# Other tiles for early weights and for the MLP's low halves in an encoder kernel

## The chip, the cores and the metric

The kernel runs on one core of a Trainium2 chip. The metric is the device time of one execution in microseconds. Five engines work side by side, each through its own queue of instructions in a fixed order: TensorE (PE, matmuls; PEld is its weight load), VectorE (DVE), ScalarE (ACT), GpSimd (POOL) and SyncE (SP), which issues most DMAs here. POOL issues some too. An instruction that waits holds up everything behind it on its engine.

## The reference

One encoder layer over two token groups (1024 and 256 tokens, 1280 in all, handled together), width 1024, all in float32:

```python
n = rms_norm(h, g_mix)
z = n @ w_in                      # columns: qa ka va (differential attention), qb kb vb (grouped queries)
oa = diff_attention(qa, ka, va)   # 4 heads, two softmax maps each, distance penalty, sub-norm
ob = gqa_attention(rope(norm(qb)), rope(norm(kb)), vb)   # 8 query heads, 2 kv heads
h = h + concat(oa, ob) @ w_out
a = relu(rms_norm(h, g_mlp) @ w_ff1); h = h + (a * a) @ w_ff2
h = h + sigmoid(rms_norm(h, g_ple) @ w_ple_gate) * (p @ w_ple_proj)
y = rms_norm(h, g_final)
```

## The kernel before, in words

Every float32 operand of a large matmul is split into a high and a low half (`hi` by a rounding copy on ACT, `lo` by a subtraction on DVE or POOL), and a product is three matmuls: high by high, high by low, low by high.

**Start.** `load_w` fetches 256 columns of `w_in` in four chunks of 256 KB (`raw`, shown as rawp in the profile), splits each (L185 on ACT, L186 on DVE), and returns the halves. Two chunks share one tile of SBUF: K0 or K1, taken in turn by the counter `raw_k`. A tile is given to its next user when its last reader is done. The first unit's weights are `w_kv`, the second's `w_va0`; later come `w_b0`, `w_va1` and one more. `load` chains its DMAs on SP: each is issued behind the one before. The chain runs: the four chunks of w_kv with pieces of x for the first 256 tokens between them (xr, and two in the tiles of xt), the four chunks of w_va0, two xt loads for the norm's statistics, two xr loads for tokens 256 to 511 (`load_x`, split at L265 and L266), then small tables. The program interleaves the matmuls of the two units, `b_unit` (psb) and `va_unit` (psv), 256 tokens at a time. Somewhat later `early_w1` uses Q0 and Q1 for the first columns of `w_ff1` (w1e).

**Attention.** Keys lie in K0, K1, Q0 and a tile of the attention pool. Finished outputs pass through the tiles o, or and ml of the pool `late`: `mixed_out` splits the last result into ml (L587 on ACT, L591 on POOL) and stores it to DRAM (md<-ml, L592). The output projection runs beside attention as side work: it loads 128 tokens of the outputs (mt<-md, L892), multiplies (pso), and adds the result to the residual (L940 on DVE). Its second half goes on when attention has ended, over four PSUM banks.

**The MLP's input.** After each norm (`mlp_norm`: L988 store, L998 to L1014) `mlp_transpose` turns 128 tokens (trn, L1103) and copies them to tiles nb (L1111 on ACT). The first matrix product of the MLP uses a scheme of seven products in place of eight, so `mlp_sums` makes seven inputs, in order 1, 6, 7, 4, 5, 2, 3: some are tiles nb as they stand, four are sums (L1135 on DVE). The first sum, t3, goes to tile T2 and the second, t2, to a tile nt; the others go to spare columns of the residual tiles (h_sb). Each input i then reaches its tile Li (`LO[i]`, shown as nlo), in one of two ways: the first groups of 128 tokens by a copy that POOL issues as DMA (L1118), later ones, from `DIRECT` on, by a split straight from the source (`n_split`, L1197 on ACT, L1198 on DVE). What was copied is split in place afterwards, by `first(i)`.

**Where tiles lie.** The pools on the left side are a stack: Q0 and Q1; then K0 and K1 (1280 words a partition each); then, during attention, `late` (o 768, or 256, ml 512 words) and the rest of the attention tiles. When attention ends, K0, K1 and all attention tiles are dropped, and the MLP's pools are stacked on the same ground: W9 (1024 words) and T2 (512), then L1 to L7 (2560 each), then W10, W11 and others. A new tile's first write waits until the tiles beneath it are done with, transfers included.

**Order.** The order of instructions on each queue is fixed when the program is built, by a simulated timeline that takes what is ready, earlier-written work first. The order written in the program is therefore not always the order on the queue, and any change of a wait can alter it elsewhere. `issue_after` holds chosen instructions behind others.

Of the kernel before, what the change touches and what calls it, by code (L numbers as in the profile page):

```python
# [14 lines left out]
F32 = mybir.dt.float32  # L15
# [8 lines left out]
P = 128  # L24
# [16 lines left out]
def f(ap):  # L41
    return ap.bitcast(F32)
# [3 lines left out]
def encoder_kernel(ctx: ExitStack, tc: tile.TileContext, x, xT, pT, w_in, w_out, w_ff1, w_ff2, w_gate, w_proj,  # L46
# [49 lines left out]
    def pool(name, bufs=1, side=None, space=None, stack=None):  # L96
        kw = dict(name=name, bufs=bufs, reuse_waits="tile")
        if side:
            kw["side"] = side
        if space:  # L100
            kw["space"] = space
        return (stack or ctx).enter_context(tc.tile_pool(**kw))
# [54 lines left out]

    w_dma = []
    raw_k = itertools.count()
    WHB = 11  # L160
    EVERY = 3
    FETCH = ((4, 6), (5, 7), (6, 2), (8, 5))
# [3 lines left out]
    def load_w(src, cols, n, rawp, wp, tag, lo_eng, between={}, dma=dma):  # L166

        c0 = cols
        hi, lo = [], []
        kn = 512 // n  # L170
        kw = {"bufs": WHB} if n == 256 else {}
        for kk in range(KD // kn):
            if kk in between:
                between[kk]()
            if n == P:
                raw = rawp.tile([P, kn, n], F32, tag="raw", name=f"raw{tag}", bufs=2)[:]
            else:

                if kk % 2 == 0:
                    raws = slot(f"K{next(raw_k) % 2}", [P, 2, kn, n], F32, f"raw{tag}")  # L180
                raw = raws[:, kk % 2]
            w_dma[:] = [dma(raw, src[kk * kn * P:(kk + 1) * kn * P, c0:c0 + n].rearrange("(k p) c -> p k c", p=P))]
            a = wp.tile([P, kn, n], F32R, tag="wh", name=f"wh{tag}", **kw)
            b = wp.tile([P, kn, n], F32R, tag="wl", name=f"wl{tag}", **kw)
            S.activation(a, raw, AF.Copy)  # L185
            lo_eng.tensor_tensor(b, raw, f(a[:]), op=ALU.subtract)  # L186
            hi += [a[:, i, :] for i in range(kn)]
            lo += [b[:, i, :] for i in range(kn)]
        return hi, lo
# [4 lines left out]
    def slot(tag, shape, dt, name):  # L194
        return slot_pool[tag].tile(shape, dt, tag=tag, name=name, bufs=1)

    def open_slots(pool_, tags):
        for tag in tags:
            slot_pool[tag] = pool_
            size = {"H": 2560, "L": 2560, "W": 1024, "Q": 1280, "K": 1280, "T": 512}[tag[0]]  # L200
            slot(tag, [P, size], F32, tag)
# [22 lines left out]
    def pj(name):  # L224
        return ppj.tile([P, 512], F32, tag="pj", name=name)
# [177 lines left out]
    def qk_a(h):  # L403

        for c, dst, sc in ((512 + P * h, kd[h], 1.0), (P * h, qd[h], -0.125 / SLOPES[h])):
            w = load_w(w_in, c, P, rawp, wp, "a", G, dma=load)
            yield from qk_unit(dst, sc, w)

    def wload(c, between={}, dma=dma):
        return load_w(w_in, c, 256, bp, bp, "p", V, between, dma)  # L410
# [541 lines left out]
    def side_work():  # L952
        yield from qk_rest()
        flush()
        open_out_proj()
        chs2 = (2, 3, 6, 7)
        ahead = []
        for ch in chs2[:2]:
            box = []
            ahead.append(lambda ch=ch: w_next.append(opw_split(opw_dma(ch))))  # L960
        yield from out_proj((0, 1, 4, 5), [], ahead, [pj], True)
        yield from out_proj(chs2, w_next, None, banks2, False)
# [63 lines left out]
    side = side_work()  # L1026
# [42 lines left out]
    pp2.append(pool("pp2", space=PSUM, bufs=1))  # L1069
    bank = lambda tag, name: pj(name) if tag == "pj" else pp2[0].tile([P, 512], F32, tag=tag, name=name, bufs=2)  # L1070
    banks2.append(lambda name: bank("f2", name))
    open_slots(pool("flz", side="left"), ["W9", "T2"])
    open_slots(pool("fl", side="left"), [f"L{i}" for i in range(1, 8)])
    HSLOT = {1: 0, 6: 1, 7: 2, 5: 3, 4: 5, 2: 6, 3: 4}
    open_slots(pool("fw", side="left"), ["W10", "W11"])
    LO = {i: slot(f"L{i}", [P, 4, HT], F32R, f"nlo{i}") for i in range(1, 8)}
# [466 lines left out]
    for ti, t in enumerate(FORD):  # L1543
# [70 lines left out]
        i = 2 if last else 1  # L1614
# [11 lines left out]
        for n0 in range(0, 512 if last else D, 512):  # L1626
            n = slice(n0, n0 + 512)
# [54 lines left out]
```

## Time and profile before

| | |
|---|---|
| median of three runs | 1716.8 us (1715.22 to 1717.41) |
| the profiled execution | 1716.65 us, of which the span is 1714.7 us |
| mean granted TensorE clock | 0.996 |
| busy share of the span | PE 97%, DVE 69%, ACT 51%, POOL 39% |
| bytes moved by DMA | 278 MB, mean 162 GB/s |

A row of the timeline reads: start in us, duration, engine, line of the program, operation, output<-inputs, shapes, count, and in brackets the time the engine stood idle before it and what ended that. A releaser is inferred: where it had long been done, another one, often a DMA, was the last. The windows give, for a stretch, the busy time of each engine, the granted clock of TensorE (1.00 is full), the mean busy share of the 16 DMA engines and the rate. The chain of waits is followed back from the last instruction.

### The profile page before, as it was taken

The numbers are of one execution on the slowest core, as the hardware profiler recorded it, in microseconds if no ns is written. First come the engines' busy times: TensorE is split into PE (matmuls) and PEld (weight loads), VectorE is DVE, ScalarE is ACT, GpSimd is POOL, SyncE is SP. The second block draws the span as 40 slices with busy tenths as digits, with TensorE's granted clock in tenths as the row PEclk, the third lists the DMA queues.
The fourth block names the chain that finished last, engine by engine and source line by source line (L and its number), as shares of the span: only waits on it lengthen the run. The fifth ranks groups of instructions, "written<-read, shape, count | busy, mean of one in ns | idle before, by whom it ended". The sixth has DMA issues, their size and how long they took to land.

```text
span 1714.7 us, 27267 instructions
## 1 busy us (share of the span) xinstructions
PE 1669.4 (97%) x9849; PEld 1490.5 (87%) x9849; DVE 1182.6 (69%) x2115; ACT 868.3 (51%) x1749; POOL 663.3 (39%) x651
## 2 busy tenths in 40 slices
PE   7999999999999999999999999999999999999997
PEld 7998888888888888879999999998888888888886
DVE  6779588778888878658766666666665865445666
ACT  7644377776766667664333333233433333354644
POOL 1124455545654345333555665520433400001441
PEclk9999999999999999999999999999999999999999
DMA  8866853432954524495443343459676366532111
GB/s 282 251 216 206 250 163 110 130 111 87 275 165 125 162 75 119 135 284 182 157 134 130 129 157 126 136 170 380 204 229 199 125 202 189 169 120 70 43 44 50
DMA packets 191866, 278.27 MB, mean 162 GB/s; under 512 B 13674, under 2 KB 121076, under 8 KB 191732
## 3 DMA queue, kind: packets, MB, share of 16 engines
q1 hardware_dynamic: 189988, 271.28, 49.7%
q0 software_dynamic: 1600, 5.24, 1.0%
q8 instruction: 78, 1.28, 0.3%
q14 instruction: 56, 0.46, 0.1%
q10 hardware_dynamic: 144, 0.00, 0.0%
HBM read 182.63 MB, written 88.61 MB: 158 GB/s over the span
## 4 chain that ended last, share of the span: by engine, by line
PE 76%; DVE 9%; ACT 4%; DMA 4%; issue 4%; POOL 3%; SPq 1%; POOLq 0%; ACTq 0%; DVEq 0%
PE psa L253 6%; PE sc L640 5%; PE av L718 5%; PE pso L253 4%; PE psb L253 4%; PE tr L694 3%; PE psv L253 2%; PE psg L1573 2%; DVE pl L705 1%; DMA xr<-in_xT 1%; DMA md<-ml 1%; DVE mm L657 1%; DVE nlo L1198 1%; PE f__16292 L156 1%; PE f__15252 L156 1%
## 5 line engine op out<-in xcount | busy, mean ns | idle before, releaser
L1370 ACT ACTIVATE ao<-ar 128x1280 fp32r<-128x1280 f32 x56 | 71.3, 1275 | 189.5 <-PE f__16296 L156 37.9
L640 PE MATMUL sc<-kt,qt 128*128 128x512 f32 (+1 forms) x576 | 156.6, 392 | 7.7 <-ACT p L665 5.1
L705 DVE TENSOR_TENSOR pl<-tr,ph 128x512 fp32r<-128x512 f32 x204 | 137.8, 684 | 32.7 <-ACT ph L700 31.4
L1372 DVE TENSOR_TENSOR ao<-ar,ao 128x1280 fp32r<-128x1280 f32 x56 | 93.3, 1666 | 92.8 <-ACT ao L1370 92.8
L700 ACT ACTIVATE ph<-tr 128x512 fp32r<-128x512 f32 x204 | 119.7, 595 | 59.0 <-PE tr L694 52.3
L253 PE MATMUL pso<-ow,mt 128*128 128x512 f32 x480 | 121.5, 399 | 5.3 <-DMA mt<-md 2.4
L694 PE MATMUL tr<-ident,p 128*128 128x128 f32 x768 | 116.0, 274 | 5.4 <-DVE pl L705 4.7
L640 PEld LDWEIGHTS sc<-kt,qt 128*128 128x128 f32 x576 | 98.9, 189 | 25.6 <-ACT p L665 6.6
L1573 PE MATMUL psg<-gw,n 128*128 128x512 f32 (+1 forms) x504 | 115.4, 384 | 0.0
L694 PEld LDWEIGHTS tr<-ident,p 128*128 128x128 f32 x768 | 91.8, 141 | 21.8 <-DVE pl L705 8.0
L253 PEld LDWEIGHTS pso<-ow,mt 128*128 128x128 f32 x480 | 88.5, 191 | 23.6 <-DVE nst L1001 2.8
L1573 PEld LDWEIGHTS psg<-gw,n 128*128 128x128 f32 x504 | 90.8, 188 | 19.5
L1091 POOL TENSOR_SCALAR w1r<-w1r,gmlp 128x256 f32<-128x256 f32 x112 | 79.4, 726 | 66.2 <-DMA w1r<-in_w_ff 41.4
L718 PE MATMUL av<-ph,vt 128*128 128x256 f32 x544 | 102.4, 289 | 0.6 <-DVE osq L745 0.4
L679 POOL TENSOR_SCALAR p<-p,rl 128x1024 f32<-128x1024 f32 x64 | 74.9, 1172 | 51.1 <-DVE rl L677 48.5
L1164 ACT ACTIVATE w<-w1s 128x512 fp32r<-128x512 f32 x56 | 35.1, 628 | 116.6 <-POOL w1s L1171 55.1
L657 DVE TENSOR_REDUCE mm<-sc 128x1 f32<-128x1024 f32 (+1 forms) x80 | 84.2, 1056 | 9.0 <-PE sc L640 8.4
L718 PE MATMUL av<-pl,vt 128*128 128x256 f32 x408 | 89.9, 302 | 0.0
L718 PEld LDWEIGHTS av<-ph,vt 128*128 128x128 f32 x544 | 82.6, 190 | 5.8 <-DVE osq L745 0.8
L665 ACT ACTIVATE p<-sc,mm 128x1024 f32<-128x1024 f32 x64 | 71.3, 1114 | 25.6 <-DVE mm L657 18.5
L653 DVE CUSTOM_DVE_ANT_0 p<-sc,dist 128x1024 f32<-128x1024 f32 x64 | 77.6, 1219 | 8.2 <-PE sc L640 3.8
L662 ACT ACTIVATE p<-p,mm 128x1024 f32<-128x1024 f32 x64 | 73.5, 1149 | 18.1 <-DVE mm L653 17.3
(1520 smaller groups left out, 4732.2 us busy)
## 6 DMA issues: line engine op xcount, KB each, us to landing
ar<-ad SPq DMA_DIRECT2D x56, 640.0 KB, 4.2
w2r<-in_w_ff SPq DMA_DIRECT2D x56, 512.0 KB, 4.6
qt<-qd SPq DMA_DIRECT2D x160, 128.0 KB, 3.2
ad<-q SPq DMA_DIRECT2D x64, 320.0 KB, 2.9
ad<-qs SPq DMA_DIRECT2D x48, 320.0 KB, 2.2
w1r<-in_w_ff SPq DMA_DIRECT2D x28, 512.0 KB, 4.3
md<-ml SPq DMA_DIRECT2D x40, 256.0 KB, 2.1
mt<-md SPq DMA_DIRECT2D x20, 512.0 KB, 5.9
```

Of the source, the lines that this page charges most:

```text
L253: PE.matmul(ps, a, b, start=i == 0, stop=i == n - 1)
L640: PE.matmul(ps[:, h0:h0 + n], shared["q"][:, cc, v, i * P:(i + 1) * P], kt[:, s0 + h0:s0 + h0 + n], start=v == 0, stop=v == 1)
L653: V.tensor_tensor_reduce(out=p[:, :sn], in0=ps[:, :sn], in1=dst_t[:, off:off + sn], scale=SLOPES[idx], scalar=3.0e38, op0=ALU.add, op1=ALU ...
L657: V.tensor_reduce(out=st["m", i][:, 0:1], in_=ps[:, :sn], axis=AX.X, op=ALU.max, negate=True)
L679: G.tensor_scalar(p[:, :sn], p[:, :sn], rl[:, 0:1], 1.0, op0=ALU.mult, op1=ALU.mult)
L694: PE.transpose(t[:, jj, i * P:(i + 1) * P], st["ws"][i][:, j * P:(j + 1) * P], ident)
L700: S.activation(ph, st["tr", j2], AF.Copy)
L705: V.tensor_tensor(pl, st["tr", j2], f(st["ph", j2][:]), op=ALU.subtract)
L718: PE.matmul(st["av"][:, :256], x_, y_, start=j2 == 0 and n == 0, stop=j2 == nj - 1 and n == len(pr) - 1)
L1091: G.tensor_scalar(raw[:, k], raw[:, k], gmlp[:, 4 * kh + k:4 * kh + k + 1], 1.0, op0=ALU.mult, op1=ALU.mult)
L1372: V.tensor_tensor(ao[:, 1], a, f(ao[:, 0]), op=ALU.subtract)
L1573: ends[:] = [PE.matmul(ps, a, b, start=m == 0, stop=m == len(pr) - 1)]
```

## The change

The first two pairs of weight units no longer alternate between K0 and K1. w_kv takes Q0 and Q1 and w_va0 takes K0 and K1; w_b0 takes Q0 and Q1 and w_va1 K0 and K1; the units after that use K0 and K1. At the end of attention, L7 is opened first and so lies where K0 and K1 were (2 x 1280 = 2560 words); W9 and T2 come next, where o, or and ml were (768 + 256 + 512 = 1536 words); L1 to L6 follow, each on the ground of the next higher one before. Before, W9 and T2 lay over K0 and the first 256 words of K1, and L1 over the rest of K1 and over o, or and ml. No computation is added or removed.

```diff
@@ -157,6 +157,8 @@
     w_dma = []
     raw_k = itertools.count()
+
+    RAWS = ("Q0", "Q1", "K0", "K1") * 2 + ("K0", "K1") * 12
     WHB = 11
@@ -177,7 +179,7 @@
                 if kk % 2 == 0:
-                    raws = slot(f"K{next(raw_k) % 2}", [P, 2, kn, n], F32, f"raw{tag}")
+                    raws = slot(RAWS[next(raw_k)], [P, 2, kn, n], F32, f"raw{tag}")
                 raw = raws[:, kk % 2]
@@ -1069,8 +1071,9 @@
     banks2.append(lambda name: bank("f2", name))
+    open_slots(pool("flk", side="left"), ["L7"])
     open_slots(pool("flz", side="left"), ["W9", "T2"])
-    open_slots(pool("fl", side="left"), [f"L{i}" for i in range(1, 8)])
+    open_slots(pool("fl", side="left"), [f"L{i}" for i in range(1, 8) if i != 7])
```

## The prediction

> **What bounds the kernel now.** I read the page first (sections 1 and 4), then TensorE's idle stretches in the timeline, then the two places the diff touches, by windows.
>
> ```profile
> span 1714.7 us, 27267 instructions
> PE 1669.4 (97%) x9849; PEld 1490.5 (87%) x9849; DVE 1182.6 (69%) x2115; ACT 868.3 (51%) x1749; POOL 663.3 (39%) x651
> ```
>
> TensorE (PE) is busy for 1669.4 of 1714.7 us, so a change can only pay where PE stands still or runs at half clock. The windows name such places; columns are the stretch, its length, busy us of PE, PEld, DVE, ACT, POOL with counts, granted clock, DMA share, GB/s.
>
> ```profile
> 3.00:8.00 5.00, 2.95 (x13) 2.66 (x13) 2.41 (x6) 3.04 (x7) 0.00 (x0) 1.00 1.00 329
> 8.00:13.00 5.00, 5.00 (x33) 4.68 (x34) 4.29 (x9) 3.93 (x8) 0.00 (x0) 1.00 0.54 163
> 13.00:23.00 10.00, 6.20 (x54) 6.00 (x52) 2.08 (x4) 3.77 (x7) 0.00 (x0) 1.00 0.99 318
> 23.00:27.00 4.00, 3.31 (x16) 3.31 (x17) 3.33 (x12) 3.86 (x11) 0.00 (x0) 0.57 0.83 299
> 60.00:70.00 10.00, 10.00 (x89) 10.00 (x87) 8.93 (x32) 6.20 (x18) 2.57 (x4) 1.00 0.72 210
> 450.00:455.00 5.00, 3.01 (x17) 2.42 (x15) 4.12 (x7) 4.72 (x10) 5.00 (x5) 0.85 0.98 329
> 700.00:705.00 5.00, 3.37 (x25) 2.80 (x23) 1.63 (x5) 3.42 (x9) 2.34 (x4) 1.00 0.15 52
> 728.00:731.00 3.00, 3.00 (x15) 2.50 (x14) 1.47 (x5) 1.55 (x5) 0.38 (x1) 1.00 0.49 162
> 734.00:736.00 2.00, 2.00 (x11) 1.58 (x11) 1.52 (x4) 0.72 (x2) 1.33 (x2) 1.00 0.23 37
> 736.00:741.00 5.00, 5.00 (x28) 4.29 (x27) 0.64 (x1) 1.30 (x4) 4.81 (x7) 1.00 0.98 344
> 750.00:755.00 5.00, 4.87 (x19) 4.06 (x20) 1.31 (x6) 1.66 (x5) 0.00 (x0) 0.66 1.06 338
> 768.00:796.00 28.00, 25.00 (x165) 23.80 (x164) 27.47 (x43) 19.87 (x34) 4.93 (x7) 1.00 0.57 181
> ```
>
> The reader should see two pairs. At the start DMA is half idle from 8 to 13 us (share 0.54), full from 13 to 23 (0.99), and PE then loses 3.8 us in 13 to 23. At the change from attention to the MLP, DMA is slack in 728 to 731 and 734 to 736 (0.49, 0.23) and overfull afterwards. PE's own rows say what each costs:
>
> ```profile
> 18.92 0.28 PE L253 MATMUL psv<-whp,xl 128*128 128x256 f32 x1
> 23.69 0.58 PE L253 MATMUL psb<-whp,xh 128*128 128x256 f32 x1 [4.49 <-ACT xh L265]
> 452.81 0.50 PE L640 MATMUL sc<-kt,qt 128*128 128x512 f32 x1 [1.99 <-ACT p L665]
> 701.71 0.70 PE L737 MATMUL av<-osq,mean_m 128*128 128x256 f32 x2 [1.57 <-ACT o L733]
> 725.64 6.06 PE L253 MATMUL pso<-ow,mt 128*128 128x512 f32 x26
> 750.13 3.03 PE L253 MATMUL pso<-ow,mt 128*128 128x512 f32 x7 [2.43 <-DMA mt<-md]
> ```
>
> So 4.49 us are lost before 23.69, and the clock is then 0.57 over four microseconds, worth another 4 x 0.43 = 1.7 us. Before 750.13 it is 2.43 us, and 5 x (1 - 0.66) = 1.7 us behind it. These four terms, 10.3 us, are what the change can reach.
>
> **Part one: raw weights of the first two units.** Before, w_kv and w_va0 both go through K0 and K1, so w_va0's first chunk waits until DVE has split w_kv's first two. All these loads are one chain on SP, and what follows (xt and xr of tokens 256 to 511) waits behind them.
>
> ```profile
> 4.31 8.04 SPq L93 DMA_DIRECT2D rawp<-in_w_in  x5
> 12.39 0.94 SPq L93 DMA_DIRECT2D xt<-in_x  x2
> 13.37 0.98 SPq L93 DMA_DIRECT2D xr<-in_xT  x2
> 13.37 9.73 DMA xr<-in_xT
> 8.57 0.87 DVE L266 SCALAR_TENSOR_TENSOR xl<-xr,gmix,xh 128x256 fp32r<-128x256 f32 x2
> 9.96 0.87 DVE L266 SCALAR_TENSOR_TENSOR xl<-xr,gmix,xh 128x256 fp32r<-128x256 f32 x2
> ```
>
> Five issues take 8.04 us, where two unblocked ones take 0.94; the fourth row, from the chain of waits, gives xr's landing at 13.37 + 9.73 = 23.10, 0.59 before PE restarts. After the change w_va0's loads go out by about 6.4. The two xt loads then wait only for their buffers, which hold x chunks until DVE's rows end at 9.44 and 10.83; xr follows at about 11.4 instead of 13.37, 2.0 us earlier. Counted in bytes: 8 to 13 would run at 318 instead of 163 GB/s, 5 x 155 = 775 KB ahead, and at 318 GB/s that is 2.4 us. I take 2.3 us off the gap, which becomes 2.2. The ends: nothing, if w_va0's megabyte, now beside the first x, only swaps places with it (PE's first 96 matmuls may then be later, but they have the gap behind them); and 4.49 if x is never late.
>
> Does the half clock stay? A gap of 1.99 us was followed by a clock of 0.85 over five microseconds, one of 1.57 by 1.00. A gap of 2.2 lies beyond the first, so I keep the penalty; its price is 1.7 or nothing. [...]
>
> The second pair (w_b0 now in Q0 and Q1, w_va1 in K0 and K1) and early_w1, whose w1e loads come behind w_b0 in Q0 and Q1, I cost at nothing: PE is busy for 10.00 of 10 us from 60 to 70. If that cover goes, the price is one wait of a load for a split, at most the 2.4 us just worked out. The small loads in the chain (gk, cs, gq) come earlier by the same 2 us.
>
> **Part two: where the MLP's tiles lie.** By the sizes in the code, L1 lay over the rest of K1 and all of the last-output tiles (o, or, ml); W9 and T2 over K0 and the start of K1. Now L7 covers K0 and K1 exactly, W9 covers o and or, T2 covers ml, and L1 to L6 move up one place, over tiles of attention's keys, values and probabilities.
>
> ```profile
> L718 PE MATMUL av<-pl,vt x408: 277/283/562, 221.0 to 718.0; 128*128 128x256 f32 x136
> 727.64 0.74 POOL L591 TENSOR_TENSOR ml<-o,ml 128x256 fp32r<-128x256 f32 x1 [5.06 <-ACT ml L587]
> 729.18 4.87 DMA md<-ml
> 734.66 0.95 POOL L1118 DMA_DIRECT2D nlo<-nb  x1 [6.28 <-DVE h_sb L940]
> 739.70 0.63 ACT L1197 ACTIVATE nhi<-nlo 128x512 fp32r<-128x512 f32 x1 [4.70 <-DMA nlo<-nb]
> 741.03 0.53 SPq L892 DMA_DIRECT2D mt<-md  x1
> mt<-md SPq DMA_DIRECT2D x1, 512.0 KB, 9.0
> DMA to landing us min/median/max: 4.2/4.9/10.9
> 723.26 0.69 DVE L1135 TENSOR_TENSOR h_sb<-nb 128x512 f32<-128x512 f32 x1 [1.89 <-ACT nb L1111]
> 723.87 0.69 DVE L1135 TENSOR_TENSOR nt<-nb 128x512 f32<-128x512 f32 x1
> 724.59 0.69 DVE L940 TENSOR_TENSOR h_sb<-pso,h_sb 128x512 f32<-128x512 f32 x1
> ```
>
> Attention's last matmul with values starts at 718.0, so what L1 to L7 now cover is free before any copy. The last ml store lands at 729.18 + 4.87 = 734.05, and POOL's first copy into L1 follows at 734.66; POOL stood 6.28 us with the other copies behind it. (The releaser named is long done; the store came last.) The copies then fill DMA from 736 on, ACT waits 4.70 for the first, and the mt load issued at 741.03 takes 9.0 us against a median of 4.9 (last figure, over mt's loads): that is the 2.43 us gap.
>
> After the change the copies into L1, L5, L2 and L3 need only the transposes' results and POOL, free at 728.4: 6.3 us earlier. Four copies of 256 KB are 1.05 MB; the slack in 728 to 731 and 734 to 736 is 3 x 0.51 + 2 x 0.77 = 3.1 us, at 344 GB/s 1.06 MB. They fit, so up to 3 us less of transfer lies before the mt load. It needs only 2.4 us. I take the gap and its half clock as gone: 2.43 + 1.7 = 4.1. The ends: nothing, since ACT freed of its 4.70 us also sends the next group's copies sooner, right against that load; and 4.1.
>
> What is late next: from 768 to 796 DVE is busy for 27.47 of 28 us and PE idles for 3.0. If PE arrives earlier, DVE must too. It was slack just before (1.31 of 5 us in 750 to 755), waiting for PE's tiles, so most of the gain passes; I take back a fifth, 0.8, with ends 0 and 4.1.
>
> What the change adds: T2 now waits for the ml store. Its first user is t3 (723.87), and t2, the fourth sum and the copies into L6, L7 and L4 follow it: three copies at 0.75 us from about 735, no later than before. Behind t3 on DVE stand the evacuations L940, which free the PSUM banks of the output projection. The order on each queue is fixed when the program is built, by readiness in a planned time: the sum at 723.26 is written after t3 and ran before it. So t3 should be placed later, and DVE held for only a little. I cost it at nothing: four banks hold four groups of 12 matmuls, 12 x 6.06 / 26 = 2.8 us each, and three of them cover 8.4 us.
>
> **The sum.** The profiled execution took 1716.65 us, span and 1.95 around it, 0.15 below the median of 1716.8. 1716.65 - 2.3 - 4.1 + 0.8 = 1711.05; I say 1711.0.
>
> **Rivals.** (a) Only the start pays: the mt load is as late as before, because the next group's copies move up against it. For it: the load was slow while those went out. It gives 1716.65 - 2.3 = 1714.4, or 1712.6 with the clock spared. (b) Only the transition pays: x lands no sooner, since DMA ran at 0.99 and w_va0's bytes must move anyway; against it, the half-idle 8 to 13. It gives 1716.65 - 3.3 = 1713.4. (c) The clock is spared at the start as well as both gains: 1711.05 - 1.7 = 1709.4; the 1.57 us gap speaks for it, the 1.99 us gap against it. [...] (d) Neither: the planner, timing everything anew, returns small waits in attention; 1716.7. (e) Slower: DVE is held at T2. If t3 keeps its place before L940's row at 724.59, DVE stands from 723.87 to 734.05, 10.2 us, 1.8 beyond the banks' 8.4, and with a half clock and the start's gain this gives 1716.65 + 1.8 + 1.7 - 2.3 = 1717.9. If the store is slowed by the new copies to the longest landing seen for mt, 10.9 us, the hold is 16.2 and the time 1723.9. [...] The 9.0 us mt load beside POOL's copies agrees. It decides against the change from a hold of 8.4 + 2.3 - 1.7 = 9.0 us on; against it is the planner's freedom.
>
> **Numbers.** Both gains, as summed: 0.33; (c) 0.15; (a) 0.25; (b) 0.06; (d) 0.11; (e) 0.10. About 0.2% (3.4 us) is what a measurement of this kernel can tell, so faster means below 1713.4: the first two cases, four tenths of (a) and some of (b), 0.60. Same: the rest of (a) and (b), and (d), 0.30. Slower: (e), 0.10. The likeliest case alone spans 1708 to 1713.4; the range, from (c) with the whole first gap gone down to 1705.5 and up over (d) to 1717.0, leaves out most of (e).
>
> **What would show it.** In the changed profile: w_va0's four issues take about 2 us, and xr of the second chunk lands near 20.8; PE's first gap is near 2.2 us; the clock in the four microseconds behind it tells (c). POOL's first copy into L1 stands near 728.4, ACT has no 4.7 us wait for it, the mt load takes 5 to 7 us and PE's wait for it is gone. DVE shows a wait at t3 for the ml store, short if the order changed. The prediction is wrong if xr lands no earlier, if the mt wait stays or moves to the next load, or if waits between 140 and 720 change by more than 2 us in sum, which no row here foretells.

## The result, and the profile after

The changed kernel takes 1706.86 us (median of five runs, 1706.03 to 1710.52) beside 1716.8 for the kernel before on the same chip (median of five, 1713.93 to 1717.41): ratio 0.995, with a 95% interval of 0.9936 to 0.9965. A ratio is worked out from all runs and need not equal that of the medians: 0.995 is a gain of 8.6 us, while the medians differ by 9.9. The forecast was 1711.0, a gain of 5.8 us. The direction was right and both places paid, and the start was worth nearly three times what the sum allowed for it.

The profiled execution after took 1706.36 us, 1704.5 of them span. The busy times from its page, then the same moments as before, read from PE's rows in the timeline:

```profile
PE 1666.3 (98%) x9849; PEld 1487.7 (87%) x9849; DVE 1183.1 (69%) x2115; ACT 868.5 (51%) x1749; POOL 664.6 (39%) x651
```

```profile
134.16 0.44 PE L341 MATMUL trb<-ident,ro 128*128 128x128 f32 x2 [0.88 <-DVE ro L318]
446.42 1.18 PE L642 MATMUL sc<-kt,qt 128*128 128x512 f32 x2 [2.12 <-ACT p L667]
689.45 1.05 PE L696 MATMUL tr<-ident,p 128*128 128x128 f32 x5 [1.09 <-DVE pl L707]
781.44 1.19 PE L156 MATMUL f__10591<-nhi,w 128*128 128x256 f32 x8 [0.51 <-DVE q L1288]
```

Before, the same four stood at these times:

```profile
140.63 0.44 PE L339 MATMUL trb<-ident,ro 128*128 128x128 f32 x2 [0.88 <-DVE ro L316]
452.81 0.50 PE L640 MATMUL sc<-kt,qt 128*128 128x512 f32 x1 [1.99 <-ACT p L665]
695.30 1.05 PE L694 MATMUL tr<-ident,p 128*128 128x128 f32 x5 [1.09 <-DVE pl L705]
791.72 1.19 PE L156 MATMUL f__10588<-nhi,w 128*128 128x256 f32 x8 [0.56 <-DVE q L1285]
```

(Lines of the changed kernel are two higher from 160 on, three higher from 1075 on.) The lead is 6.47 us at 134, 6.39 at 446, 5.85 at 689 and 10.28 at 781. So the start brought 6.5, attention gave 0.6 back, the transition brought 4.4, and from there to the end the lead stays (the spans differ by 10.2).

How it looks where the change acts: SP's issues at the start, ACT's first split of the late xr, and the windows.

```profile
4.31 3.17 SPq L93 DMA_DIRECT2D rawp<-in_w_in  x5
11.18 0.98 SPq L93 DMA_DIRECT2D xr<-in_xT  x2
xr<-in_xT SPq DMA_DIRECT2D x2, 512.0 KB, 6.6
17.56 1.29 ACT L267 ACTIVATE xh<-xr,gmix 128x256 fp32r<-128x256 f32 x3
8.00:13.00 5.00, 5.00 (x35) 4.77 (x36) 4.87 (x10) 4.54 (x10) 0.00 (x0) 1.00 1.08 378
13.00:23.00 10.00, 10.00 (x87) 10.00 (x87) 6.41 (x21) 8.32 (x21) 0.60 (x2) 1.00 0.93 349
23.00:28.00 5.00, 5.00 (x44) 5.00 (x44) 4.20 (x20) 5.00 (x18) 1.23 (x3) 1.00 1.01 341
```

From 8 to 13 us DMA now moves 378 GB/s instead of 163. xr is issued at 11.18 and its two transfers take a median of 6.6 us (before, 9.7). ACT splits the first of them from 17.56 on (before, from 23.13), so it is there when PE wants it. PE is busy for all 20 us from 8 to 28, the 4.49 us gap is gone, and so is the half clock behind it (1.00 from 23 on, where it was 0.57).

The transition: POOL's copies, t3, the mt load, and two windows.

```profile
716.32 2.44 POOL L1121 DMA_DIRECT2D nlo<-nb  x3
718.76 0.75 POOL L1121 DMA_DIRECT2D nlo<-h_sb  x1
720.86 0.74 POOL L593 TENSOR_TENSOR ml<-o,ml 128x256 fp32r<-128x256 f32 x1 [1.35 <-ACT nst L1004]
728.10 0.68 DVE L942 TENSOR_TENSOR h_sb<-pso,h_sb 128x512 f32<-128x512 f32 x1
728.76 0.69 DVE L1138 TENSOR_TENSOR nt<-nb 128x512 f32<-128x512 f32 x1
734.76 0.52 SPq L894 DMA_DIRECT2D mt<-md  x1
mt<-md SPq DMA_DIRECT2D x1, 512.0 KB, 7.1
715.00:760.00 45.00, 45.00 (x232) 38.65 (x231) 27.97 (x65) 31.75 (x70) 15.93 (x22) 1.00 0.96 311
757.70:785.70 28.00, 24.57 (x161) 23.14 (x160) 26.83 (x44) 19.56 (x33) 4.87 (x7) 1.00 0.52 168
```

Four copies go out from 716.32 on, ahead of even the last ml sum at 720.86; before, the first one went at 734.66. The mt load takes 7.1 us instead of 9.0. From 715 to 760 PE has no idle time, and no half clock stands there (clock 1.00). The last row is the stretch that was 768 to 796 before (the same work, 10.3 us earlier): there DVE was busy for 27.47 us and PE for 25.00, and now it is 26.83 and 24.57.

### The profile page after: what moved, and what is told of

Its sections match the earlier page's. It is cut to its first block, busy times and chain, and to the rows that moved or that the text cites. A ratio compares the mean times of both kernels' runs of the same rounds, so it can differ in the third digit from the quotient of the medians.

```text
span 1704.5 us, 27269 instructions
## 1 busy us (share of the span) xinstructions
PE 1666.3 (98%) x9849; PEld 1487.7 (87%) x9849; DVE 1183.1 (69%) x2115; ACT 868.5 (51%) x1749; POOL 664.6 (39%) x651
## 4 chain that ended last, share of the span: by engine, by line
PE 78%; DVE 8%; ACT 4%; issue 4%; POOL 3%; DMA 3%; SPq 0%; POOLq 0%; ACTq 0%; DVEq 0%
PE psa L255 6%; PE sc L642 5%; PE av L720 5%; PE psb L255 4%; PE pso L255 4%; PE tr L696 4%; PE psv L255 3%; PE psg L1576 2%; DVE pl L707 1%; PE f__16295 L156 1%; PE f__15255 L156 1%; PE f__16637 L156 1%; PE f__15600 L156 1%; PE f__15937 L156 1%; PE f__14906 L156 1%
```

## Experiments

The runs fall in two groups, each with its own runs of the kernel before on the same chip: 1718.67 us median (17 runs) for the first four, 1716.58 (27 runs) for the last four. Gains are given by the ratios. A profile is one execution, and single executions of one kernel lie up to 8.6 us apart (1709.6 to 1718.2 in experiment 1), so a profile shows where time goes, and the ratio what it is worth.

**1. The start alone.** The four raw tiles of the change, the MLP's tiles as before.

```diff
+    RAWS = ("Q0", "Q1", "K0", "K1") * 2 + ("K0", "K1") * 12
-    raws = slot(f"K{next(raw_k) % 2}", ...
+    raws = slot(RAWS[next(raw_k)], ...
```

> The raw-weight tiles of part one alone; the MLP's tiles lie as before. My theory after seeing the changed kernel: the start gives 6.5 us (first gap 4.49 and its half clock 1.7 gone), attention returns about 0.6, and the 2.43 us gap before the late mt load with its half clock stays: 5.9 us less than before, about 1711. Rival: the two parts act only together (the transition gap closes because all comes 6 us earlier), then it gives about 10 us, 1707. Second rival, the predicted size: 2.3 us, 1714.4.

1713.57 us, ratio 0.9974 (0.9962 to 0.9987): about 4.5 us less. The gap at 19 is gone, the one for mt is not. This profile shows a new loss, in its waits from 60 to 72 us:

```profile
DVE lam_p L448 <- DMA lam_t<-in_lams: 3.0, 1, 3.0
PE psb L255 <- DVE rr L149: 2.8, 1, 2.8
```

DVE stands 3.0 us for a small load, the norm's rr is queued behind it, and PE loses 2.8 us. The profile after has no PE wait there, with the same raw tiles. DVE waits for lam_t in each of the ten profiles, for 0.5 to 3.2 us (2.6 before), and in the others PE stands still for little of it or nothing; here the norm's rr was placed behind the wait. So the loss is one of the order on DVE's queue. That the second pair of raw tiles brings it isn't shown: no run changes the start without that pair and leaves the MLP's tiles as they were.

**2. The tiles alone.**

```diff
+    open_slots(pool("flk", side="left"), ["L7"])
     open_slots(pool("flz", side="left"), ["W9", "T2"])
-    open_slots(pool("fl", side="left"), [f"L{i}" for i in range(1, 8)])
+    open_slots(pool("fl", side="left"), [f"L{i}" for i in range(1, 8) if i != 7])
```

> The move of L7, W9 and T2 of part two alone; raw weights as before. Theory: POOL's first copy no longer waits for the last ml store, the mt load lands in time, the 2.43 us gap and its half clock go: about 4.3 us less, 1712.5, with the first gap of 4.49 us still there. If attention's small return of 0.6 us comes from the changed start, it is absent here. Rival: the copies, moved ahead alone, run against the mt load and the gap stays: 1716.8.

1712.19 us, ratio 0.9968 (0.9955 to 0.998): about 5.5 us less. The mt gap is gone; the first gap stays, and here a half clock twice as long follows it:

```profile
23.25 0.58 PE L253 MATMUL psb<-whp,xh 128*128 128x256 f32 x1 [4.06 <-ACT xh L265]
21.48:28.31 6.83, 5.07 (x23) 5.07 (x24) 5.25 (x19) 5.88 (x18) 0.78 (x2) 0.50 0.91 329
```

The product of the two ratios is 0.9942, the whole change 0.995 (0.9936 to 0.9965): within the intervals the two parts add.

**3. Only the first pair.** The whole change, with the second pair back on K0 and K1.

```diff
-    RAWS = ("Q0", "Q1", "K0", "K1") * 2 + ("K0", "K1") * 12
+    RAWS = ("Q0", "Q1", "K0", "K1") + ("K0", "K1") * 14
```

> The changed kernel with Q0 and Q1 for the first unit only; w_b0 and w_va1 use K0 and K1 in turn as before. Theory: the second pair is hidden under a busy PE, so 1706.9 within 1 us. Rival: the second pair brings part of the gain or of the return in attention; then it differs by 1 us or more.

1708.85 us, ratio 0.9948 (0.9936 to 0.9961), not to be told from the whole change. As far as the intervals tell, all of the start's gain lies in w_kv and w_va0.

**4. T2 off the stored tile.** The whole change, with T2 and W9 exchanged, so that T2 no longer lies over the ml tiles.

```diff
-    open_slots(pool("flz", side="left"), ["W9", "T2"])
+    open_slots(pool("flz", side="left"), ["T2", "W9"])
```

> The changed kernel with T2 and W9 swapped, so that T2 lies over the first words of o and W9 over the rest of o, or and ml. T2 no longer waits for the last ml store; t3 (728.8 in the changed kernel) can run near 722. Theory: that wait is placed late by the plan and costs nothing, so 1706.9 within 1 us. Rival: the copies into L6, L7 and L4 that follow t3 come earlier and relieve the busy DMA, 1 to 2 us less.

1709.28 us, ratio 0.9953 (0.9939 to 0.9967): the same. T2's new wait costs nothing that can be measured. Nor did it put t3 late: t3 (the row of nt below) keeps its place here, some 10 us behind POOL's first four copies.

```profile
715.10 2.45 POOL L1121 DMA_DIRECT2D nlo<-nb  x3
717.54 0.75 POOL L1121 DMA_DIRECT2D nlo<-h_sb  x1
727.75 0.69 DVE L1138 TENSOR_TENSOR nt<-nb 128x512 f32<-128x512 f32 x1
```

**5. Is it the order of the loads, or the bytes?** The kernel before, with xr of the second chunk issued ahead of xt of the first.

```diff
-    stats_x(0, 256, load)
     load_x(256, 256, dma=load)
+    stats_x(0, 256, load)
```

> The kernel before with one pair of lines exchanged: the second chunk's xr is issued ahead of the first chunk's xt; raw weights and the MLP's tiles as before. It asks what held xr at the start. Theory 1 (xr stands in SP's queue behind the blocked raw loads, and behind xt): xr is issued about 1 us earlier, at 12.4 instead of 13.37, since the raw loads still block until 12.35, and lands by about 1 us earlier, at 22; the gap at 19.2 shrinks from 4.49 to about 3.5, the clock stays at half for a window, time 1 us less (0.9994, not to be told from no change). Theory 2 (bytes: xr's landing is set by the megabytes issued ahead of it and beside it): the megabyte of xt leaves xr's way, at 318 to 370 GB/s up to 3 us; gap at most 1.5, no half clock, time 4 to 5 us less (0.997). Rival: whatever is issued before the landing takes its share anyway, so nothing moves and the gap stays at 4.5 (1.000).

1719.01 us, ratio 1.0011 (1.0001 to 1.0021): no gain. Yet xr did come early. The chain of waits, the windows, and the rows that now wait:

```profile
12.12 5.89 DMA xr<-in_xT
8.00:13.00 5.00, 5.00 (x31) 4.78 (x31) 4.27 (x9) 3.70 (x8) 0.00 (x0) 1.00 0.57 180
13.00:23.00 10.00, 10.00 (x88) 10.00 (x87) 4.91 (x11) 6.23 (x13) 0.00 (x0) 1.00 0.92 319
28.00:36.00 8.00, 6.21 (x49) 6.00 (x48) 3.21 (x14) 4.40 (x15) 0.46 (x1) 0.94 0.85 295
24.99 0.47 ACT L383 ACTIVATE vl<-psv,rstd 128x256 fp32r<-128x256 f32 x1 [0.88 <-DVE rstd L149]
26.04 0.39 PE L253 MATMUL psv<-whp,xh 128*128 128x256 f32 x1 [0.99 <-DVE vl L384]
33.76 0.39 PE L253 MATMUL psb<-whp,xh 128*128 128x256 f32 x1 [1.79 <-ACT xh L265]
```

xr lands 5.89 us after its issue at 12.12, that is at 18.0 instead of 23.1, even earlier than theory 2 has it, and the gap at 19 is gone. But xt lands later, the first at 20.6 instead of 19.0. ACT's vl waits for the row statistics that come from xt, PE waits for vl, and then for the third chunk's xr. Up to 50 us PE stands still for 4.1 us (idle stretches over 0.25 us, the first wait left out) where before it stood for 4.5, and a half clock follows in both (0.94 from 28 to 36 us here, 0.57 from 23 to 27 before). From 8 to 13 us DMA is as idle as before (0.57), and from 13 to 23 it moves 319 GB/s where it moved 318: as many bytes arrive by then, and their order chose who waits. So theory 2 was right on xr and wrong on the time. What the raw tiles give beyond an earlier xr is the transfer that fills 8 to 13.

**6. Another lo tile over the outputs.** The kernel before, with L3 in L1's place.

```diff
-    open_slots(pool("fl", side="left"), [f"L{i}" for i in range(1, 8)])
+    open_slots(pool("fl", side="left"), [f"L{i}" for i in (3, 1, 2, 4, 5, 6, 7)])
```

> The kernel before with the seven lo tiles opened in the order 3, 1, 2, 4, 5, 6, 7: L3 instead of L1 lies over the rest of K1 and the last outputs; no tile is moved elsewhere, W9 and T2 stay over K0. Theory (POOL's copies queue behind the first one that waits for the last ml store): the copies into L1, L5 and L2 go as soon as POOL's outputs are done, near 716 to 722, only the one into L3 waits until about 734; the mt load takes about 7 instead of 9.0 us and its gap of 2.43 with the half clock behind it is gone: 4 to 6.5 us less (0.997), as with the tiles alone moved. Rival: the copy into L3 stands at the head of POOL's queue by then and holds what follows (L6, L7, L4) to the same time as before, so the copies still go out beside the mt load; the gap of 2.4 stays and the time is the same (1.000).

1714.42 us, ratio 0.9989 (0.998 to 0.9998): about 2 us, not the 5.5 of experiment 2. The timeline, a row of POOL's waits and the DMA issues at the end:

```profile
726.13 0.95 POOL L1118 DMA_DIRECT2D nlo<-nb  x1
736.92 1.50 POOL L1118 DMA_DIRECT2D nlo<-nb  x2 [6.12 <-DMA md<-ml]
759.22 1.18 POOL L1118 DMA_DIRECT2D nlo<-nb  x1 [1.49 <-ACT nb L1111]
768.76 0.66 PE L1103 MATMUL trn<-ident,hn 128*128 128x128 f32 x4 [3.04 <-ACT nb L1111]
771.92 2.93 PE L156 MATMUL f__10453<-nhi,w 128*128 128x384 f32 x8 [2.51 <-ACT nhi L1197]
ACT nhi L1197 <- DMA nlo<-nb: 3.6, 1, 3.6
757.51 3.17 SPq L970 DMA_DIRECT2D w<-wed  x4
nlo<-nb POOLq DMA_DIRECT2D x1, 256.0 KB, 8.3
```

The copies start at 726.13 and the mt gap is gone, as the theory said. The rival's mechanism is there too: POOL stands 6.12 us for the store. And a new loss follows: the last copy of a group goes at 759.22, behind the first of four 512 KB weight loads, and takes 8.3 us. ACT waits 3.6 for it and PE 3.04 + 2.51, and the matmuls behind these waits are slow: eight of 128x384 take 2.93 us at 771.92, where eight took 1.55 at 763.03. With the tiles alone moved (experiment 2) the same copy goes out ahead of those four loads and takes 4.7; ACT then waits 2.4 for it, and PE 1.1 + 0.9:

```profile
758.25 0.75 POOL L1119 DMA_DIRECT2D nlo<-nb  x1 [5.14 <-ACT nb L1112]
759.01 3.08 SPq L970 DMA_DIRECT2D w<-wed  x4
nlo<-nb POOLq DMA_DIRECT2D x1, 256.0 KB, 4.7
```

So the gain of the tiles isn't only the one load of mt: with no lo tile over ml, the whole row of copies is placed earlier, and this one goes ahead of the weight loads further on.

**7. Both cheap reorderings, 5 and 6 together.**

> Both of the two reorderings of this call together (xr ahead of xt; L3 over the last outputs), without the four raw tiles and without new places for W9, T2 and L7. If the effects add, the ratio is the product of the two: 0.994 if both pay (1707), 0.997 if the tiles alone do. Rival: a planner that times everything anew returns some us in attention, as in the kernel with the start alone changed, where a wait for lam_t cost 2.8 us.

1718.34 us, ratio 1.001 (1.0001 to 1.0019). The product of their ratios is 1.0000, within what their intervals allow. Neither reordering, nor both together, replaces its part of the change.

**8. The start with L3 over the outputs.** The change's raw tiles with experiment 6's order.

> The changed kernel's four raw tiles at the start together with the order 3, 1, 2, 4, 5, 6, 7 of the lo tiles; W9, T2 and L7 stand as in the kernel before. If only POOL's first copies matter, it equals the changed kernel: 0.9945, about 1707. If T2 over the ml tile costs something that this avoids (its wait for the store), it is 1 to 2 us faster; if the copy into L3 waiting for the store until 734 holds the last copies, 2 to 4 us slower (1709 to 1711).

1711.18 us, ratio 0.9964 (0.9951 to 0.9978); the product of experiments 1 and 6 is 0.9963. That is 0.0014 above the change's ratio, but the two intervals overlap, so it isn't shown to be slower. Its profile, of the slowest of the five executions (1715.77), has the waits of experiment 6 again, 3.4 us of PE at 770 and 2.2 at 773. No version tried is measurably faster than the change.

## Why the prediction was right, and where its size was off

- **The start: 2.3 us forecast, 6.5 measured.** This is the mis-sized term. The step that failed is "2.3 us off the gap, which becomes 2.2": it turned the filled window into 775 KB, with 8 to 13 running at the old 318 GB/s, and it took that or the earlier issue, not both. DMA ran at 378, so (378 - 163) x 5 us = 1.08 MB came early, an estimate of 3.1 us at the 349 GB/s of the stretch behind it, and xr was issued 2.2 us earlier (11.18 for 13.37). ACT splits it from 17.56 instead of 23.13, 5.6 us earlier, which covers the whole 4.49. How much each of the two gave isn't separated by any run. I had put the whole gap at the far end of the range's working, as "x is never late".
- **The half clock at the start: forecast to stay, gone.** It went with the gap and was worth 1.7 us; 4.49 and 1.7 are 6.2 of the 6.5. Rival (c), both gains with the clock spared, is what happened, and I had given it 0.15. Its 1709.4 was still too high because it kept a gap of 2.2 us. The likeliest case, with a span of 1708 to 1713.4, did not happen.
- **The second pair at nothing:** right for the whole change (experiment 3). Whether it has a part in the 2.8 us of experiment 1 is open.
- **The transition: 4.1 less 0.8 forecast, 4.4 measured.** The gap of 2.43 and its half clock went as summed, but by another way: I kept POOL's old order and expected the copies from 728.4 on, in the slack of 728 to 736; they came from 716.32 on, ahead of the last ml sum, because the order was made anew. In the stretch where I feared for DVE, it is still the bound, and PE stands still for 0.4 us more than before (28 less 24.57, against 28 less 25.00): the give-back was half of the 0.8. The rest isn't a gain of the tiles: the wait of 1.57 at 701.71 is no longer there, and 0.75 of it comes back at the next transposes. The same exchange, 1.6 for about 0.7, stands in every profile with a changed start and in none with the old one (rows below), so it comes with the start. No row before the change foretold it, and that it makes up for the smaller losses is luck.
- **T2's wait: nothing, as forecast.** Rival (e) needed t3 in its old place before a row of the output sums; t3 stands right behind one, at 728.76, without a wait. Experiment 4 shows that this place is not the doing of T2's wait; the new order as a whole put it there.
- **Rivals (a) and (b)** are refuted by experiments 1 and 2: each part pays alone, and they add. **(d)**, small waits returned in attention, is there with 0.6 us.

At the transition, with the start alone changed (experiment 1) and with the tiles alone changed (experiment 2):

```profile
700.89 1.34 PE L696 MATMUL tr<-ident,p 128*128 128x128 f32 x7 [0.73 <-DVE pl L707]
701.24 0.70 PE L737 MATMUL av<-osq,mean_m 128*128 128x256 f32 x2 [1.59 <-ACT o L733]
```

The leads add up to 1716.65 - 6.5 + 0.6 - 4.4 = 1706.4, as they must; the profiled execution took 1706.36. By cause, 6.2 of the start and 2.43 + 1.7 + 0.8 - 0.4 = 4.5 of the transition are named above. That the gain is just the 10.3 us of the four terms that the prediction called within reach is a coincidence, since the 0.8 us gained elsewhere nearly offsets the 0.6 and the 0.4. The lower end of the range, 1705.5, was worked out nowhere: all four terms with nothing taken back give 1706.3.

These terms are read from one execution each. The first gap is 4.49 us in the profile before, but 4.06 and 3.37 in those of experiments 2 and 6, whose start is the same.

Open: why DMA moved 318 GB/s at a share of 0.99 in the old stretch and 349 at 0.93 in the new one. The mix of transfers differs, and no run here separates that. Also open is what the planner would do with lam_t loaded earlier; that was not tried.

## What to carry to other kernels

When a load is late, look for an idle stretch of DMA ahead of it and ask what holds the queue there. Filling that stretch paid here (378 GB/s instead of 163 from 8 to 13 us, and a start 6.5 us shorter), while reordering the same bytes moved the wait to whoever was then last (4.1 us of PE's waits up to 50 us in experiment 5, 4.5 before). A tile laid over a buffer that a late store still reads can hold more than its own copy: in experiment 6 POOL stood 6.12 us for the store, and the tile also set where the copies behind it went. Price a gap of TensorE with its clock: here, where a gap went whole, the half clock behind it went too (the gaps of 4.49 and 2.43 us, each with 1.7 us behind it).

## What the runs showed of the hardware

In the kernel before, the half clock came in three stretches of 3.41 us between its first matmuls and its end. They begin at 23.43, 453.51 and 750.47 us, that is 430.08 and 296.96 us apart, 126 and 87 times 3.413. The changed kernel has one, at 446.49, and in experiment 2 one lasted 6.83 us. Two stretches of 3.41 us, one after the other, from each of four kernels: the kernel before, the changed one, experiment 7 and experiment 1:

```profile
747.06:750.47 3.41, 0.98 (x5) 0.52 (x4) 1.21 (x6) 3.15 (x8) 1.42 (x2) 1.00 1.07 309
750.47:753.88 3.41, 3.41 (x12) 2.75 (x11) 0.84 (x3) 0.72 (x2) 0.00 (x0) 0.50 1.02 356
```

```profile
443.08:446.49 3.41, 1.29 (x12) 1.08 (x10) 3.11 (x5) 3.00 (x7) 3.41 (x3) 1.00 0.96 300
446.49:449.90 3.41, 3.41 (x11) 2.88 (x12) 2.06 (x4) 2.99 (x7) 3.41 (x4) 0.50 1.05 373
```

```profile
22.84:26.25 3.41, 1.80 (x16) 1.59 (x14) 0.82 (x5) 2.01 (x6) 0.00 (x0) 1.00 0.76 206
26.25:29.66 3.41, 2.82 (x23) 2.82 (x24) 3.28 (x14) 2.86 (x9) 2.04 (x4) 1.00 0.48 166
```

```profile
742.31:745.72 3.41, 2.17 (x10) 1.47 (x8) 1.65 (x3) 2.87 (x7) 1.71 (x3) 1.00 1.02 260
745.72:749.13 3.41, 2.11 (x11) 1.79 (x12) 1.93 (x7) 1.99 (x7) 0.75 (x1) 1.00 1.02 346
```

A stretch with PE busy for 0.98 or 1.29 of 3.41 us was followed by one at 0.50. With 1.80 busy the clock stayed at 1.00, and so it did over a gap of 2.5 us that lies across two such stretches, 2.17 and 2.11 busy. The length of a gap alone doesn't tell the two apart: gaps of 1.99 and 2.43 us in the kernel before and of 2.12 in the changed one had the half clock behind them, gaps of 2.21 us in experiment 7 (ahead of 26.84) and of 2.5 and 2.8 us in experiment 1 (the second ahead of 67.86) had not. So a gap of 2 to 2.5 us cost itself alone or 1.7 us more (half of 3.41). That its place decides is my estimate from these four pairs; no run moves a gap to test it. The 2.2 us that the prediction left of the first gap lie in that range, so the price it weighed there, 1.7 or nothing, was open. The wait near 450 us, which no version touches, brought a half clock before and after (at 453.51 and 446.49), so its 1.7 us are in both profiles.

By the spacing of its matmuls the kernel also begins at half clock, which the windows don't show: their clock is 1.00 up to 9.78 us in the profile before, where the trace's records of the clock begin. Up to 9.78 matmuls of 128x256 start 0.21 us apart, as they do again in the half-clock stretch from 23.43 on, and behind 9.78 they start 0.12 apart. The spacing changes at 9.78 us before, 13.65 us ahead of 23.43, at 9.6 in the changed kernel and near 11 in experiment 5.
